# Adding adaLN's partial sums over partitions by accumulating transfers instead of TensorE matmuls

## The chip, the cores and the metric

The kernel runs on one core of a Trainium2 chip. The metric is the device time of one execution in microseconds. Before the change three runs took 1121.29 to 1122.57 us, with a median of 1122.05 us. Times inside an execution come from one profiled execution and are counted from the start of its span.

## What is computed

The kernel computes a two-layer trunk for 512 tokens of width 1024, all in float32. Layer 0 is stick-breaking attention and a SwiGLU FFN, layer 1 a gMLP token mixer and a second SwiGLU FFN. Each of the four sub-layers is wrapped in two RMS norms and in an adaLN modulation by one conditioning vector `c`:

```python
def ada_modulation(c, w, b):
    m = jax.nn.silu(c) @ w + b
    shift, scale, gate = jnp.split(m, 3, axis=-1)
...
    shift, scale, gate = ada_modulation(c, mix_ada_w[i], mix_ada_b[i])
    h = rms_norm(x, mix_pre_g[i]) * (1.0 + scale) + shift
    y = mixer(h)
    x = x + gate * rms_norm(y, mix_post_g[i])
```

So each sub-layer s needs three rows of 1024 numbers from `c`, each a product of a vector of 1024 with a 1024 x 1024 matrix. The code names them after the sub-layer whose residual they follow: G0 to G3 are the gates of sub-layers 0 to 3 (times `post_g`), A0 to A2 the scales (one plus scale, times `pre_g`) of sub-layers 1 to 3, and B0 to B2 their shifts. G0 belongs to attention, G1 to FFN 0, G2 to gMLP and G3 to FFN 1; A1 and B1 are used at the end of FFN 0 for gMLP's input, A2 and B2 at the end of gMLP for FFN 1's input. (The scale and shift of attention itself are made in another way, at the start.)

## The kernel before

**Matmuls.** Every float32 matrix is split into a high and a low part (`split`): ScalarE copies the high part to fp32r, VectorE subtracts it from the source. `mm3` (line 90 is the matmul in it) then does three matmuls, high by high, high by low, low by high. So each weight tile of 128 x 1024 goes by DMA into `raw`, through a copy on ScalarE (`wh`) and a subtraction on VectorE (`wl`), and activations go the same way (`as` in front of the projections back). Nearly all compute instructions on VectorE and ScalarE are recorded through one helper, so that they carry line 64.

**Stages.** Attention ends near 260 us of the span. FFN 0 follows: three plain units (`gu`), nineteen blocks by seven products instead of eight (`r`), then the projection back, `out_proj`, with 22 weights of `wdown` (`y`), of which the last four are the tail. gMLP comes next (`u` units, eight steps of `v` for each of two halves, the last four of the second half in the tail, the layer norm, three more `u` units, the mixing over positions `sv`, `out_proj`), and FFN 1 last, whose projection back is written out in `last` (`X`, `M`). At the end of each `out_proj`, `boundary` does for each of four token tiles the norm, the gate (`t<-y,G`), the residual, which POOL stores to DRAM (`xd`), and the next input (`t<-x,A`, then `t<-t,r,B`), which TensorE transposes (`tp`).

**The adaLN rows.** Class `Bg` makes the rows in the background, one step at a time, in between the steps of the stages. For each row, POOL clears an accumulator of 128 x 1024 and SP loads the bias into its first partition. Then eight times a slab of 128 x 1024 of the matrix is loaded (`rawada`) and VectorE adds it, scaled by the slab's part of silu(c), in one instruction (`ada_stt`). After this, the 128 partitions of the accumulator hold partial sums. They are added over the partitions, and the sum brought to all partitions, on TensorE: each half of 512 is split (`acch` on ScalarE, `accl` on VectorE), multiplied by a matrix of ones (`adaps`), and evacuated with the multiplication by a broadcast `pre_g` or `post_g`, or copied for B:

```python
split(h[:], l[:], acc[:, c])
...
ps = self.bank()
mm(ps[:], ones_r, h[:], True, False, last_tp[0])
mm(ps[:], ones_r, l[:], False, True)
```

Attention sums G0, A0 and B0 in that way with slabs that POOL loads. G1 is made in FFN 0's blocks and G3 in FFN 1's, with slabs in slots of the pool `s4`. A1, B1 and G2 are made in FFN 0's `out_proj`, two slabs a weight, with two slab buffers that they share with the FFN blocks' `rawy`. When their 24 slabs are through, at k = 13 (`mid`), the bank of token tile 0 is copied to SBUF (`yp`), so that `adaps` gets a bank, all three rows are added over partitions there, and token tile 0 begins anew in the bank; `yp` is added at its end. From k = 13 on the A2 and B2 object takes one step a weight, and it is finished in gMLP's `v` steps, two slabs a step.

**What sets the order.** Each engine runs its instructions in order, and so do the DMA queues of SP and POOL: an instruction whose wait is not over holds all behind it. From FFN 0 on no order is written out by hand for VectorE, ScalarE and SP. A scheduler of the tile framework sets it when the program is built, from the order of the code and from its own estimates. `Written.gate` and `order` add constraints to it.

Of the kernel before, what the change touches and what calls it, by code (L numbers as in the profile page):

```python
# [8 lines left out]
F32 = mybir.dt.float32  # L9
# [16 lines left out]
def trunk(ctx: ExitStack, tc: tile.TileContext, A: dict, out: bass.AP):  # L26
# [5 lines left out]
    adas = ctx.enter_context(tc.tile_pool(name="adas", bufs=1))  # L32
# [3 lines left out]
    dram = ctx.enter_context(tc.tile_pool(name="dram", bufs=1, space=bass.MemoryType.DRAM))  # L36
    psum = ctx.enter_context(tc.tile_pool(name="psum", bufs=1, space=bass.MemoryType.PSUM))

    uid = [0]
# [264 lines left out]
    lng = cols[:, 1, :]  # L304

    def ada_stt(acc, w, kk):
        dve.scalar_tensor_tensor(
            acc, w, sc[:, kk : kk + 1], acc, ALU.mult, ALU.add
        )

# [2 lines left out]
    class Bg:  # L313
# [4 lines left out]

        def __init__(self, *parts, slots=False, queue=nc.sync):
            self.slots = slots  # L320
            self.queue = queue
            self.bank = lambda: bank("adaps", "p")
# [15 lines left out]
        def run(self):  # L338
            for name, at, s, part in self.parts:
                acc = slot(F32, name, 1, D)[:, 0, :]  # L340
                ada[name, at] = acc
                nc.gpsimd.memset(acc, 0.0)
                load(acc[0:1, :], A["adab"][s, part], self.queue)
                for k in range(KD):
                    if self.slots:
                        raw = slot(F32, "rawada", 1, D)[:, 0, :]
                        load(raw, A["ada"][s, part, k])
                        yield
                    else:
                        self.ahead(1 + (k + 1 < KD or name != self.parts[-1][0]))  # L350
                        raw = self.raws.pop(0)
                    ada_stt(acc, raw, k)
                    if not self.slots:
                        yield
            for name, at, s, part in self.parts:
                acc = ada[name, at]
                if part:
# [3 lines left out]
                for b in range(2):  # L361
                    c = slice(b * 512, (b + 1) * 512)
                    h = adas.tile([P, 512], F32R, tag="acch", name=nm("acch"))
                    l = adas.tile([P, 512], F32R, tag="accl", name=nm("accl"))
                    split(h[:], l[:], acc[:, c])
                    yield
                    yield
                    ps = self.bank()
                    mm(ps[:], ones_r, h[:], True, False, last_tp[0])
                    mm(ps[:], ones_r, l[:], False, True)  # L370
                    if part == 0:
                        act.activation(acc[:, c], ps[:], AF.Copy)
                    elif part == 1:
                        dve.scalar_tensor_tensor(acc[:, c], ps[:], 1.0, g[:, c], ALU.add, ALU.mult)
                    else:
                        dve.tensor_tensor(acc[:, c], ps[:], g[:, c], ALU.mult)

        def step(self, n=1):

            while n and next(self.gen, self) is not self:  # L380
                n -= 1
            return n

    def rms(part, first=None):

# [104 lines left out]
        return t  # L490


    def out_proj(s, nk, get_act, wkey, J, bg, hT, nxt=(), pre=None, S=None, steps=0, bg2=None):

        last = 0 if steps else 3
        mid = min(nk - J, -(-8 * len(bg.parts) // steps) + 1) if steps else None  # L500
        yp = None
        y = [[None, None] for _ in range(NT)]

        def step(k, tt, a, w, halves=(0, 1)):
            for hf in halves:
                if k == 0 or k == mid and tt == last:
                    y[tt][hf] = bank("y", "p" if tt == last else "b")
                mm3(
                    y[tt][hf][:],
                    a[0][:, tt * P : (tt + 1) * P], a[1][:, tt * P : (tt + 1) * P],  # L510
                    w[0][:, 0, hf * 512 : (hf + 1) * 512],
                    w[1][:, 0, hf * 512 : (hf + 1) * 512],
                    k == 0 or k == mid and tt == last, k == nk - 1 or k + 1 == mid and tt == last,
                )

        npre = 0
# [26 lines left out]
        for tt in range(NT):  # L543
            for hf in range(2):
                for k, a, w in tail:
                    step(k, tt, a, w, (hf,))
            if tt == last and yp is not None:
                for hf in range(2):
                    dve.tensor_tensor(yp[:, hf, :], y[tt][hf][:], yp[:, hf, :], ALU.add)
                y[tt] = [yp[:, hf, :] for hf in range(2)]  # L550
# [208 lines left out]
    with tc.tile_pool(name="att", bufs=1) as att, tc.tile_pool(name="att2", bufs=6) as att2:  # L759
# [192 lines left out]
        bg.bank = None  # L952
        cur = attend(0)
        for k in range(KD):
            if k % 2 == 0:
# [18 lines left out]
        for i in range(NPAIR):  # L974
# [6 lines left out]
            def rest():  # L981
                n, sums = next(F)
                fill(n)
                bg.step(sums)

            for group, js in zip((LATE, *EARLY), (B31, B2, B0)):
                flip(group, 0)
# [11 lines left out]
                step_v(i - 2)  # L999
        for _ in fgen:  # L1000
            bg.step(1)
        bg.step(99)
        pe["chain"] = dve.chain = act.chain = False

# [14 lines left out]
    class Ffn:  # L1019
# [78 lines left out]

            return rest

        def run(self, bg0, bg, bg2, steps, nhT, nxt, nS=None):
            for f in range(NH):
                self.unit(f, 256, 256)()
            for f in range(NH, KF):
                self.seven(f)()
                if f % 3:
                    bg0.step(1)
            bg0.step(99)
            if self.li == 1:
                return self.last()  # L1110
            out_proj(
                self.s, KF, lambda k: act_split(self.act[k // 2][:, k % 2, :]),
                lambda k: ("wdown", self.li, k), 4, bg, nhT, nxt, None, nS, steps, bg2,
            )


        def last(self):
# [113 lines left out]
            for half in range(2):  # L1231
# [3 lines left out]
                tail = items[-NLAST:] if half else []  # L1235
                while n < len(items) and items[n][0] == half and items[n] not in tail:
                    ahead(n)
                    _, kind, j = items[n]
                    n += 1
                    if kind == "o":  # L1240
# [75 lines left out]
        return lambda: [e() for e in ev]  # L1316

    def gmlp(bg, hT, nhT, nS, nxt):
        wsr = wraw.tile([P, KD, P], F32, tag="raw", name="wsr")
        load(wsr[:], A["ws"])  # L1320
        nc.gpsimd.memset(wsr[0:64, :, 64:P], 0.0)
# [93 lines left out]
                    )  # L1415

        for m in range(KD):
            mix(m)
            sp.append(act_split(u4[m // 2][:, m % 2, :]))
            if m >= 4:  # L1420
# [12 lines left out]
    )  # L1433
    bg2 = Bg("A2", "B2")
    f0.run(
        Bg("G1", slots=True), Bg("A1", "B1", "G2"), bg2, 2, hT2,
        [lambda a=a: u_first(hT2, range(a, min(a + 2, NU))) for a in range(0, NU, 2)],
    )
    gmlp(bg2, hT2, hT3, S3, f1.first())
    f1.run(Bg("G3", slots=True), bg2, None, 0, None, ())  # L1440


def _layout(i):
# [82 lines left out]
```

## Time and profile before

| what | value |
|---|---|
| median of three runs | 1122.05 us |
| the profiled execution | 1123.81 us |
| its span | 1122.0 us |
| TensorE busy | 1104.4 us, 7318 matmuls |
| VectorE busy | 903.3 us, 1161 instructions |
| ScalarE busy | 603.4 us, 977 instructions |
| POOL busy | 39.8 us, 71 instructions |
| rawada loads on SP's queue | 56 of 512 KB, 4.7 us each from issue to landing |
| rawada loads on POOL's queue | 24 of 512 KB, 4.5 us each |

Matmuls are pipelined and their ends are modelled, so the length of one in a row is longer than the distance to the next one. PE is TensorE, PEld its weight loads, DVE VectorE, ACT ScalarE; SPq and POOLq are the queues on which SP and POOL issue DMAs. A row of a timeline has the start, the length, the engine, the line, the operation with its output and inputs by the program's names, and, in brackets, idle time before it and what ended that.

### The profile page before, as it was taken

What the parts mean: (1) busy time and instruction counts of PE and PEld (TensorE: products, weight loads), DVE (VectorE), ACT (ScalarE), POOL (GpSimd) and SP (SyncE); (2) the same over time, 40 slices, a digit from 0 to 9 for tenths busy, and PEclk for the clock granted to TensorE, in tenths of its full rate; (3) what the DMA queues carried; (4) which work ended last, traced back from release to release, by engine and by line L of the source; (5) the groups of instructions that cost most, each with busy time, mean ns of one, the idle gap of its engine ahead of it and who ended that gap; (6) DMA issues with size and microseconds to landing.
All of it is one profiled execution on the core that took longest, in us unless ns stands there. A gap on an engine that the chain in (4) does not pass through costs nothing.

```text
span 1122.0 us, 18286 instructions
## 1 busy us (share of the span) xinstructions
PE 1104.4 (98%) x7318; PEld 993.9 (89%) x7318; DVE 903.3 (81%) x1161; ACT 603.4 (54%) x977; POOL 39.8 (4%) x71
## 2 busy tenths in 40 slices
PE   6999999999999999999999999999999999999997
PEld 5788878779999999988878988989999999989896
DVE  7777889759998988797587774759988988889986
ACT  7646767646655555552244634437555555556552
POOL 0220111000000000010000000000000000000000
PEclk9999999999999999999999999999999999999999
DMA  9676445353344444278874582333244444223223
GB/s 358 229 228 169 142 147 160 135 188 132 106 125 147 151 148 122 90 243 264 272 255 167 182 286 80 110 129 134 77 151 140 128 133 147 76 75 113 95 96 149
DMA packets 51298, 176.09 MB, mean 157 GB/s; under 512 B 5643, under 2 KB 6155, under 8 KB 50318
## 3 DMA queue, kind: packets, MB, share of 16 engines
q1 hardware_dynamic: 45166, 153.95, 42.0%
q0 software_dynamic: 6048, 20.98, 6.0%
q8 instruction: 57, 0.93, 0.3%
q14 instruction: 27, 0.22, 0.1%
HBM read 164.43 MB, written 8.39 MB: 154 GB/s over the span
## 4 chain that ended last, share of the span: by engine, by line
PE 88%; DMA 6%; DVE 3%; ACT 2%; issue 1%; SPq 0%; DVEq 0%; ACTq 0%
PE r L90 33%; PE y L90 12%; PE X L90 7%; PE v L90 7%; PE pqk L90 7%; PE gu L90 6%; PE u L90 4%; DMA rawada<-in_ada 3%; PE M L90 3%; PE z L90 2%; PE av L90 2%; PE tw L98 2%; DMA raw<-in_wdown 1%; DMA ada<-in_ada0w 1%; PE tp L98 1%; PE sv L90 1%
## 5 line engine op out<-in xcount | busy, mean ns | idle before, releaser
L64 ACT ACTIVATE wh<-raw 128x1024 fp32r<-128x1024 f32 (+1 forms) x112 | 117.0, 1051 | 138.3 <-PE y L90 45.6
L64 DVE TENSOR_TENSOR wl<-raw,wh 128x1024 fp32r<-128x1024 f32 (+1 forms) x112 | 135.0, 1211 | 59.4 <-ACT wh L64 57.9
L90 PE MATMUL r<-Sh,wh 128*128 128x256 f32 x608 | 170.2, 280 | 0.3 <-ACT e L64 0.3
L90 PE MATMUL r<-Sh,wl 128*128 128x256 f32 x608 | 170.4, 280 | 0.0
L90 PE MATMUL r<-Sl,wh 128*128 128x256 f32 x608 | 170.1, 280 | 0.0
L90 PE MATMUL y<-wh,as 128*128 128x512 f32 x480 | 154.0, 398 | 0.0
L64 DVE TENSOR_TENSOR wl<-f,wh 128x1024 fp32r<-128x1024 f32 x76 | 92.8, 1220 | 35.8 <-ACT wh L64 35.8
L64 ACT ACTIVATE wh<-f 128x1024 fp32r<-128x1024 f32 x76 | 80.7, 1061 | 67.9 <-PE r L90 64.8
L90 PEld LDWEIGHTS r<-Sh,wh 128*128 128x128 f32 x608 | 114.7, 189 | 0.5 <-ACT e L64 0.5
L90 PEld LDWEIGHTS r<-Sl,wh 128*128 128x128 f32 x608 | 114.6, 189 | 0.0
L90 PEld LDWEIGHTS r<-Sh,wl 128*128 128x128 f32 x608 | 114.6, 189 | 0.0
L90 PEld LDWEIGHTS y<-wh,as 128*128 128x128 f32 x480 | 90.7, 189 | 21.3
L90 PE MATMUL y<-wl,as 128*128 128x512 f32 x240 | 95.5, 398 | 0.0
L90 PE MATMUL r<-hTh,wh 128*128 128x256 f32 x304 | 88.8, 293 | 0.0
L90 PE MATMUL r<-hTl,wh 128*128 128x256 f32 x304 | 84.8, 279 | 0.0
L90 PE MATMUL r<-hTh,wl 128*128 128x256 f32 x304 | 80.1, 280 | 0.0
L90 PE MATMUL X<-wh,as 128*128 128x512 f32 (+1 forms) x272 | 76.2, 356 | 0.0
L64 ACT ACTIVATE e<-r 128x256 f32<-128x256 f32 x114 | 43.4, 382 | 51.9 <-PE r L90 51.7
L90 PEld LDWEIGHTS r<-hTh,wh 128*128 128x128 f32 x304 | 57.2, 188 | 5.1 <-DVE gu L64 0.9
L90 PE MATMUL r<-hTh,b 128*128 128x256 f32 x304 | 60.7, 282 | 0.0
L64 ACT ACTIVATE wh<-rawx 128x1024 fp32r<-128x1024 f32 x38 | 40.4, 1062 | 36.5 <-PE r L90 30.8
L90 PEld LDWEIGHTS r<-hTl,wh 128*128 128x128 f32 x304 | 57.3, 188 | 0.1
(240 smaller groups left out, 2842.6 us busy)
## 6 DMA issues: line engine op xcount, KB each, us to landing
rawada<-in_ada SPq DMA_DIRECT2D x56, 512.0 KB, 4.7
raw<-in_wdown SPq DMA_DIRECT2D x44, 512.0 KB, 4.0
rawy<-in_wy SPq DMA_DIRECT2D x38, 512.0 KB, 3.6
rawx<-in_wx SPq DMA_DIRECT2D x38, 512.0 KB, 4.3
rawada<-in_ada POOLq DMA_DIRECT2D x24, 512.0 KB, 4.5
raw<-in_wqk SPq DMA_DIRECT2D x16, 512.0 KB, 4.2
ada<-in_ada0w SPq DMA_DIRECT2D x7, 1026.0 KB, 11.2
raw<-in_wgu SPq DMA_DIRECT2D x12, 512.0 KB, 3.5
```

Source lines behind the costliest of these rows:

```text
L64: b = f(*a, **k)
L90: b = nc.tensor.matmul(o, l, r, start=start, stop=stop, skip_group_check=True)
L98: last_tp[0] = nc.tensor.transpose(o, i, ident)
```

## The change

The code of `Bg` now keeps the matmuls for G0, A0 and B0 alone. When the last slab of any other row is added, a generator `total` is appended to a list `trees`; each call of `grow` takes every generator in it one step further. `total` adds partitions 64 to 127 onto 0 to 63 by a DMA that accumulates, then 32 to 63 onto 0 to 31, and so on: seven DMAs on POOL's queue, each of which needs the one before. Then VectorE multiplies the one row that is left in partition 0 by `pre_g` or `post_g` (not for B), and POOL writes the row to DRAM and loads it from there into all partitions.

Calls of `grow` are put where steps of the stages are: in `Bg.step`, in `run`, in `last`, in the mixing loop and in `out_proj`. With no `adaps` in FFN 0's `out_proj`, `mid`, `yp` and the second object (`bg2`) go from it: its steps are two slabs a weight for k < 8, one after that. A2 and B2 are summed in gMLP alone, behind the last `t<-t,r,B` of the boundary before (`bg.gate`). The pool `adas` of the split halves moves behind the others in SBUF.

```diff
-                    ada_stt(acc, raw, k)
+                    b = ada_stt(acc, raw, k)
+                    if self.gate is not None:
+                        order(b, self.gate)
+                    if k == KD - 1 and self.queue is nc.sync:
+                        trees.append(total(acc, s, part))
                     if not self.slots:
                         yield
+            if self.queue is nc.sync:
+                return
...
             while n and next(self.gen, self) is not self:
+                grow()
                 n -= 1
             return n
+
+    trees = []
+
+    def total(acc, s, part):
+
+        n = P // 2
+        while n:
+            nc.gpsimd.dma_start(out=acc[0:n, :], in_=acc[n : 2 * n, :], accum_op=ALU.add)
+            yield
+            n //= 2
+        if part:
+            g = slot(F32, "g", 1, D)[:, 0, :]
+            load(g[0:1, :], A["pre_g" if part == 1 else "post_g"][s : s + 1, :], nc.gpsimd)
+            yield
+            if part == 1:
+                dve.scalar_tensor_tensor(acc[0:1, :], acc[0:1, :], 1.0, g[0:1, :], ALU.add, ALU.mult)
+            else:
+                dve.tensor_tensor(acc[0:1, :], acc[0:1, :], g[0:1, :], ALU.mult)
+        row = dram.tile([1, D], F32, tag="row", bufs=4, name=nm("row"))
+        nc.gpsimd.dma_start(out=row[:], in_=acc[0:1, :])
+        yield
+        nc.gpsimd.dma_start(out=acc, in_=row[:].to_broadcast([P, D]))
+
+    def grow(n=1):
+
+        while n and trees:
+            trees[:] = [t for t in trees if next(t, trees) is not trees]
+            n -= 1
...
-            bg.step(steps)
-            if bg2 is not None and mid is not None and k >= mid:
-                bg2.step(1)
-            if k + 1 == mid:
-                yp = slot(F32, "yp")
-                for hf in range(2):
-                    act.activation(yp[:, hf, :], y[last][hf][:], AF.Copy)
-                bg.step(99)
+            bg.step(steps if k < KD else min(steps, 1))
+            if steps == 0:
+                grow()
...
     def gmlp(bg, hT, nhT, nS, nxt):
+        bg.gate = ready[0]
```

Three pieces of the order show what moves. The first is ScalarE's in FFN 0's `out_proj`; `raw` to `wh` are weights, `as` activation splits. Before, from the sixteenth to the eighteenth weight of `wdown`:

```order
L64 ACTIVATE wh_5661<-raw_5659 128x1024
L64 ACTIVATE wh_5749<-raw_5747 128x1024
L64 ACTIVATE wh_5792<-raw_5790 128x1024
L64 ACTIVATE yp_5695<-y_5180 128x512
L64 ACTIVATE yp_5695<-y_5184 128x512
L64 ACTIVATE as_5744<-act_4044 128x512
L64 ACTIVATE as_5787<-act_4294 128x512
L64 ACTIVATE as_5823<-act_4294 128x512
L64 ACTIVATE as_5859<-act_4544 128x512
L64 ACTIVATE as_5895<-act_4544 128x512
L64 ACTIVATE as_5931<-act_4798 128x512
L64 ACTIVATE as_5952<-act_4798 128x512
```

Now, from the ninth weight to the fourteenth; after these rows come weights alone up to the boundary:

```order
L64 ACTIVATE as_5840<-act_4544 128x512
L64 ACTIVATE wh_5385<-raw_5383 128x1024
L64 ACTIVATE as_5873<-act_4792 128x512
L64 ACTIVATE as_5894<-act_4792 128x512
L64 ACTIVATE as_5897<-act_5036 128x512
L64 ACTIVATE wh_5426<-raw_5424 128x1024
L64 ACTIVATE as_5900<-act_5036 128x512
L64 ACTIVATE wh_5467<-raw_5465 128x1024
L64 ACTIVATE wh_5512<-raw_5510 128x1024
L64 ACTIVATE wh_5553<-raw_5551 128x1024
L64 ACTIVATE wh_5590<-raw_5588 128x1024
```

The copies into `yp` and the splits of accumulators are gone, and the activation splits, of which seven stood in a row behind the eighteenth weight, are all through before the eleventh.

The second is POOL's in the same stage. Before, its instructions for A1, B1, G2 and A2 and the first store of the residual:

```order
L342 MEMSET A_5212 128x1024
L342 MEMSET B_5373 128x1024
L342 MEMSET G_5532 128x1024
L342 MEMSET A_5779 128x1024
L429 DMA xd_6006<-x_5962 128x1024
```

Now, from the middle of B1's tree (B_5369; A_5196 is A1, G_5540 is G2, `row` a row in DRAM):

```order
L395 DMA B_5369<-B_5369 32x1024
L407 DMA row_5504<-A_5196 16x1x64
L395 DMA B_5369<-B_5369 16x1024
L409 DMA A_5196<-row_5504 128x1024
L395 DMA B_5369<-B_5369 8x1024
L395 DMA B_5369<-B_5369 4x1024
L395 DMA B_5369<-B_5369 2x1024
L395 DMA G_5540<-G_5540 64x1024
L395 DMA B_5369<-B_5369 1x16x64
L395 DMA G_5540<-G_5540 32x1024
L407 DMA row_5769<-B_5369 16x1x64
L395 DMA G_5540<-G_5540 16x1024
```

B1's last addition stands behind G2's first one, which waits for G2's last slab; the stores of the residual stand behind all of G2's additions.

The third is VectorE's in gMLP, around the statistics of the layer norm (`bns`, `mv`); `wl` are weights. Before:

```order
L64 TENSOR_TENSOR wl_6803<-raw_6800,wh_6802 128x1024
L64 TENSOR_TENSOR accl_6751<-B_6583,acch_6750 128x512
L64 TENSOR_TENSOR wl_6809<-raw_6806,wh_6808 128x1024
L64 TENSOR_TENSOR wl_6905<-raw_6902,wh_6904 128x1024
L64 BN_STATS bns_6812<-vt_6524 128x6
L64 BN_AGGR mv_6813<-bns_6812 128x2
L64 BN_STATS bns_6812<-vt_6525 128x6
L64 BN_AGGR mv_6813<-bns_6812 128x2
L64 BN_STATS bns_6812<-vt_6526 128x6
L64 BN_AGGR mv_6813<-bns_6812 128x2
L64 TENSOR_TENSOR wl_6961<-raw_6958,wh_6960 128x1024
```

Now, with B2's sixth to eighth slabs and A2's multiply by `pre_g`:

```order
L64 SCALAR_TENSOR_TENSOR B_6603<-rawada_6653,sc,B_6603 128x1024
L64 TENSOR_TENSOR wl_6856<-raw_6853,wh_6855 128x1024
L64 SCALAR_TENSOR_TENSOR B_6603<-rawada_6657,sc,B_6603 128x1024
L64 BN_STATS bns_6763<-vt_6464 128x6
L64 SCALAR_TENSOR_TENSOR B_6603<-rawada_6673,sc,B_6603 128x1024
L64 BN_AGGR mv_6764<-bns_6763 128x2
L64 BN_STATS bns_6763<-vt_6465 128x6
L64 BN_AGGR mv_6764<-bns_6763 128x2
L64 SCALAR_TENSOR_TENSOR A_6502<-A_6502,g_6676 1x1024
L64 BN_STATS bns_6763<-vt_6466 128x6
L64 BN_AGGR mv_6764<-bns_6763 128x2
L64 TENSOR_TENSOR wl_6912<-raw_6909,wh_6911 128x1024
```

The last two slabs and the multiply now stand among the second half's statistics, where only weights stood.

More of the change, by code (lines that the diff above doesn't have):

```diff
@@ L31, in trunk @@
     wpool = ctx.enter_context(tc.tile_pool(name="wpool", bufs=5))
-    adas = ctx.enter_context(tc.tile_pool(name="adas", bufs=1))
     npool = ctx.enter_context(tc.tile_pool(name="npool", bufs=2))
@@ L36, in trunk @@
     dram = ctx.enter_context(tc.tile_pool(name="dram", bufs=1, space=bass.MemoryType.DRAM))
+    adas = ctx.enter_context(tc.tile_pool(name="adas", bufs=1))
     psum = ctx.enter_context(tc.tile_pool(name="psum", bufs=1, space=bass.MemoryType.PSUM))
@@ L306, in ada_stt @@
     def ada_stt(acc, w, kk):
-        dve.scalar_tensor_tensor(
+        return dve.scalar_tensor_tensor(
             acc, w, sc[:, kk : kk + 1], acc, ALU.mult, ALU.add
@@ L320, in __init__ @@
             self.slots = slots
-            self.queue = queue
-            self.bank = lambda: bank("adaps", "p")
+            self.queue, self.gate, self.turn = queue, None, 0
             self.parts = [
@@ L368, in run @@
                     ps = self.bank()
-                    mm(ps[:], ones_r, h[:], True, False, last_tp[0])
+                    mm(ps[:], ones_r, h[:], True, False)
                     mm(ps[:], ones_r, l[:], False, True)
@@ L490, in x_load, with out_proj @@
         return t
-    def out_proj(s, nk, get_act, wkey, J, bg, hT, nxt=(), pre=None, S=None, steps=0, bg2=None):
+    def out_proj(s, nk, get_act, wkey, J, bg, hT, nxt=(), pre=None, S=None, steps=0):
         last = 0 if steps else 3
-        mid = min(nk - J, -(-8 * len(bg.parts) // steps) + 1) if steps else None
-        yp = None
         y = [[None, None] for _ in range(NT)]
@@ L505, in step @@
             for hf in halves:
-                if k == 0 or k == mid and tt == last:
+                if k == 0:
                     y[tt][hf] = bank("y", "p" if tt == last else "b")
@@ L512, in step @@
                     w[1][:, 0, hf * 512 : (hf + 1) * 512],
-                    k == 0 or k == mid and tt == last, k == nk - 1 or k + 1 == mid and tt == last,
+                    k == 0, k == nk - 1,
                 )
@@ L546, in out_proj @@
                     step(k, tt, a, w, (hf,))
[L547 to L550, printed above, removed]
             if tt < 2:
@@ L983, in rest @@
                 fill(n)
-                bg.step(sums)
+                if bg.step(sums):
+                    grow()
             for group, js in zip((LATE, *EARLY), (B31, B2, B0)):
@@ L1001, in trunk @@
             bg.step(1)
+            grow()
         bg.step(99)
@@ L1099, in seven, with run @@
             return rest
-        def run(self, bg0, bg, bg2, steps, nhT, nxt, nS=None):
+        def run(self, bg0, bg, steps, nhT, nxt, nS=None):
             for f in range(NH):
@@ L1107, in run @@
                     bg0.step(1)
+                else:
+                    grow()
             bg0.step(99)
@@ L1112, in run @@
                 self.s, KF, lambda k: act_split(self.act[k // 2][:, k % 2, :]),
-                lambda k: ("wdown", self.li, k), 4, bg, nhT, nxt, None, nS, steps, bg2,
+                lambda k: ("wdown", self.li, k), 4, bg, nhT, nxt, None, nS, steps,
             )
@@ L1237, in last @@
                     ahead(n)
+                    grow()
                     _, kind, j = items[n]
@@ L1417, in gmlp @@
         for m in range(KD):
+            grow()
             mix(m)
@@ L1435, in trunk @@
     f0.run(
-        Bg("G1", slots=True), Bg("A1", "B1", "G2"), bg2, 2, hT2,
+        Bg("G1", slots=True), Bg("A1", "B1", "G2"), 2, hT2,
         [lambda a=a: u_first(hT2, range(a, min(a + 2, NU))) for a in range(0, NU, 2)],
@@ L1439, in trunk @@
     gmlp(bg2, hT2, hT3, S3, f1.first())
-    f1.run(Bg("G3", slots=True), bg2, None, 0, None, ())
+    f1.run(Bg("G3", slots=True), bg2, 0, None, ())
 def _layout(i):
```

1 line of the change is left out of this document (removed).

## The prediction

> **What bounds the kernel now.** I read the page's busy times first, then what TensorE waited for, then TensorE in order of time around the one wait that I found, then the chain behind that wait.
>
> ```profile
> span 1122.0 us, 18286 instructions
> PE 1104.4 (98%) x7318; PEld 993.9 (89%) x7318; DVE 903.3 (81%) x1161; ACT 603.4 (54%) x977; POOL 39.8 (4%) x71
> ```
>
> TensorE is busy 98% of the span, so a change pays by the matmuls that it takes from TensorE and by the waits that it ends there. The list of TensorE's waits has one in the middle of the kernel that belongs to the code that is changed, and the group view gives the matmuls that go:
>
> ```profile
> PE adaps L90 <- ACT acch L64: 2.0, 1, 2.0
> L90 PE MATMUL adaps<-acch,ones x14: 387/396/549, 465.7 to 996.7; 128*128 128x512 f32 x14
> L90 PE MATMUL adaps<-accl,ones x14: 392/392/628, 465.9 to 997.0; 128*128 128x512 f32 x14
> ```
>
> That is 7 rows (G1, A1, B1, G2, A2, B2, G3) by 2 halves by 2 matmuls, 28 in all. The 0.39 us of one is not what it costs: matmuls overlap. TensorE in order of time (start, length) in FFN 0's projection back shows the spacing, and the wait:
>
> ```profile
> 560.76 0.39 PE L90 MATMUL adaps<-acch,ones 128*128 128x512 f32 x1
> 560.99 0.40 PE L90 MATMUL adaps<-accl,ones 128*128 128x512 f32 x1
> 561.23 0.40 PE L90 MATMUL y<-wh,as 128*128 128x512 f32 x1
> ...
> 562.39 0.62 PE L90 MATMUL y<-wh,as 128*128 128x512 f32 x2
> 565.02 0.50 PE L90 MATMUL adaps<-acch,ones 128*128 128x512 f32 x1 [2.01 <-ACT acch L64]
> ...
> 569.00 0.63 PE L90 MATMUL y<-wh,as 128*128 128x512 f32 x2
> ```
>
> A 512-wide matmul starts 0.233 us after the one before it (560.76 to 561.23 is two). At 565.02 TensorE had stood 2.01 us, and from 565.02 to 569.00 ten matmuls start in 3.98 us, 0.40 each. The windows view says why: the clock column falls below 1.00 (columns: window, length, busy of PE, PEld, DVE, ACT and POOL, clock, DMA share, GB/s).
>
> ```profile
> 482.00:560.00 78.00, 78.00 (x362) 64.06 (x361) 57.92 (x57) 25.70 (x36) 2.87 (x3) 1.00 0.82 264
> 560.00:580.00 20.00, 17.99 (x71) 14.09 (x71) 18.60 (x25) 10.06 (x18) 0.00 (x0) 0.91 0.77 256
> ```
>
> The chain that ended last tells what the awaited `acch` stood behind on ScalarE: a weight that came late, two copies into `yp`, seven activation splits and one more weight.
>
> ```profile
> 550.39 1.23 DVE wl L64
> 551.64 6.09 DMA raw<-in_wdown
> 557.84 1.06 ACT wh L64
> 558.90 0.97 ACT yp L64 x2
> 559.87 3.27 ACT as L64 x7
> 563.40 1.05 ACT wh L64
> ```
>
> **What the change takes from TensorE.** 28 matmuls by 0.233 us are 6.5 us. The wait at 565.02 is a wait of a matmul that no longer exists: 2.01 us from the modelled end of the matmul before, and 0.17 us more since the next start normally falls before that end (0.40 long, 0.233 apart): 2.2 us. The slow stretch behind it costs 3.98 less 10 by 0.233, 1.65 us. Sum: 6.5 + 2.2 + 1.65 = 10.4 us.
>
> [...]
>
> What could be late next at that place are the weights and the activation splits. The split at 550.39 is the sixteenth of `wdown` in VectorE's order, for k = 15; TensorE starts k = 13 at 561.23 and takes 24 by 0.233 = 5.6 us for one k, so it wants k = 15 at 572: 20 us of lead. The activation splits now stand far ahead in ScalarE's order, all before the eleventh weight. So I put nothing in the place of this wait. The two adds into `yp` leave the boundary's chain as well, for which TensorE does not wait: nothing.
>
> **What it adds, and what hides it.** Each row gets seven dependent accumulating transfers on POOL's queue, a multiply on one partition (not B), a write to DRAM and a broadcast load. No accumulating transfer is in the trace. The nearest rows of POOL's queue, from issue to landing:
>
> ```profile
> A<-in_adab POOLq DMA_DIRECT2D x1, 4.0 KB, 2.4
> xd<-x POOLq DMA_DIRECT2D x12, 512.0 KB, 2.9
> after<-V POOLq DMA_DIRECT2D x4, 508.0 KB, 10.4
> g<-in_post_g SPq DMA_DIRECT2D x4, 512.0 KB, 7.3
> ```
>
> The bounds of one step are 2.4 and 10.4 us. I take 2.9: the steps have 256 KB falling to 4 KB, and only `after`, SBUF to SBUF as these are but queued five in a row behind a slab, is slow. A tree is then 7 by 2.9 = 20 us, and 2.9 + 7.3 = 10 us more until all partitions have the row. Nothing of it is on TensorE; the question is who is behind it on VectorE, which works in order. The rows that set the dates:
>
> ```profile
> 506.52 1.28 DVE L64 SCALAR_TENSOR_TENSOR A<-rawada,sc,A 128x1024 f32<-128x1024 f32 x1
> 533.66 1.28 DVE L64 SCALAR_TENSOR_TENSOR G<-rawada,sc,G 128x1024 f32<-128x1024 f32 x1 [0.64 <-DMA rawada<-in_ada]
> 555.15 1.28 DVE L64 SCALAR_TENSOR_TENSOR G<-rawada,sc,G 128x1024 f32<-128x1024 f32 x1 [1.15 <-DMA rawada<-in_ada]
> 606.16 1.28 DVE L64 SCALAR_TENSOR_TENSOR t<-t,r,B 128x1024 f32<-128x1024 f32 x1
> 1028.36 0.42 DVE L64 TENSOR_TENSOR tf<-tf,raw 128x256 f32<-128x256 f32 x1
> 1056.97 1.29 DVE L64 TENSOR_TENSOR K<-K,G 128x512 f32<-128x512 f32 x2
> ```
>
> A1: the last slab is added by 507.8, the multiply stands behind G2's first slab (534.9): 27 us for seven steps, 3.9 each. Behind it wait G2's slabs and the weights for k = 13 and on, with the 20 us of lead. B1: its last step stands on POOL behind G2's first, which waits for G2's last slab (556.4); a step, the row's write and the broadcast end near 556 + 2.9 + 2.9 + 7.3 = 570, wanted at 606 less the gain so far. G3's multiply stands behind the sum at 1028.36, 28 us ahead of its use, and the row's write and broadcast need 10. The x stores behind the trees on POOL are read a stage later. The memsets of the accumulators, for which SP's loads of `adab` wait, stand on POOL ahead of the trees of their stage. All these I cost at nothing; with a cover gone, each us late would be one of TensorE's. The multiply is no row of the trace: between a one-column operation and the 1.28 us of 128 partitions I take the latter; five of them replace ten evacuations and fourteen low-part splits, so VectorE and ScalarE have less to do.
>
> **The moved slabs.** A2 and B2 are now all summed in gMLP: sixteen slabs where eight were. Two buffers pace them. VectorE's rows of before for the eight and for the layer norm behind them, and TensorE's step that needs the norm (times here are before's):
>
> ```profile
> 644.88 2.60 DVE L64 SCALAR_TENSOR_TENSOR B<-rawada,sc,B 128x1024 f32<-128x1024 f32 x2
> 652.39 2.61 DVE L64 SCALAR_TENSOR_TENSOR B<-rawada,sc,B 128x1024 f32<-128x1024 f32 x2 [1.39 <-DMA rawada<-in_ada]
> 658.43 2.60 DVE L64 SCALAR_TENSOR_TENSOR B<-rawada,sc,B 128x1024 f32<-128x1024 f32 x2
> 665.08 2.60 DVE L64 SCALAR_TENSOR_TENSOR B<-rawada,sc,B 128x1024 f32<-128x1024 f32 x2 [0.80 <-DMA rawada<-in_ada]
> ...
> 688.60 0.69 DVE L64 BATCH_NORM_STATS2 bns<-vt 128x6 f32<-128x512 f32 x1 [1.11 <-ACT vt L64]
> 689.32 0.21 DVE L64 BATCH_NORM_AGGREGATE mv<-bns 128x2 f32<-128x12 f32 x1
> 698.05 1.21 DVE L64 TENSOR_TENSOR wl<-raw,wh 128x1024 fp32r<-128x1024 f32 x1
> 699.56 0.18 DVE L64 RECIPROCAL r<-sd 128x4 f32<-128x4 f32 x1 [0.30 <-ACT sd L64]
> 706.75 2.36 DVE L64 TENSOR_TENSOR vnl<-vt,vnh 128x1024 fp32r<-128x1024 f32 x2 [0.59 <-ACT vnh L64]
> ...
> 713.28 6.65 PE sv L90 x60
> ```
>
> Pairs come 6.73 us apart (20.20 by 3), and with one weight a pair, as at 533.66 to 555.15, 6.14 apart. Four gaps of the latter and three of the former put the eighth pair at 689.6, with one BN_STATS inside it to 692.9. In the order there follow A2's multiply, three more statistics, four aggregates and two weights (1.28 + 3 by 0.69 + 4 by 0.21 + 2 by 1.21 = 6.6 us), to the reciprocal at 699.5, where it was. The layer norm then ends at 709.1, and TensorE, eight matmuls (1.9 us) shorter here, wants it at 711.4: 2.3 us to spare. Cost nothing, thinly covered. A2's tree starts near 668, and its multiply stands behind the eighth pair: 25 us, 3.6 for a step.
>
> **Against the profiled execution** (1123.8, its span 1122.0) the sum gives 1113.4; that run was 1.75 above the median of the three (1122.05), so the median to expect is 1111.7.
>
> **Rivals.** First, the layer norm comes late. At the slowest distance of the rows, 7.5 us (644.88 to 652.39), the eighth pair ends at 700.7, the norm 7.7 us later than worked out, 5.4 beyond the cover; with a slow stretch of 1.65 us that takes 7 us back: 1118.7. For it: the cover is 2.3 us; against: the slab pace slows with the number of weights loaded between, and there are fewer. Chance 0.15.
>
> Second, the wait at 565 stays under another name, or was not in the timed runs: then only the matmuls count, 1115.5. For it: ScalarE waited for a weight there. Against: the lead of 20 us. Chance 0.08.
>
> Third, slower: the steps of the trees are slow. VectorE's multiply for A2 then holds the layer norm, and all of the lateness reaches TensorE. It costs from 3.6 us a step on; lateness is 7 by (d - 3.6) less 2.3 of cover, plus 1.65. At d = 5.2 the 10.4 us are spent; at d = 6 it is 16.8 - 2.3 + 1.65 = 16.2, so 1128; at 10.4 us the multiply for A1 breaks its lead of 20 us too (73 - 27 - 20 = 26), near 1185. For it: the row of `after`, the only transfer within SBUF, and that an accumulating one must read what it adds to. Against: the rows of 2.4 and 2.9. Chance 0.08. [...]
>
> That the matmuls don't go is none: the built program has 28 fewer.
>
> **The numbers.** Forecast 1111.7 at 0.66; with 0.15 and 0.08 for the first two rivals, 0.08 for the third, 0.03 left for small losses that leave no change. About 0.2%, 2.2 us, is what a measurement of this kernel can tell: faster is below 1119.8. The worst of the first rival lies near that, so faster 0.87, same 0.05, slower 0.08. The range reaches down by the spread of the runs (1121.3 to 1122.6) and the rounding of the terms to 1110, and up to the first rival's bulk, 1118; the third is left out.
>
> **What would show it.** Right: no `adaps` among TensorE's groups, no TensorE wait near 555 to 570, clock 1.00 in that window, `sv` straight behind `u`, POOL's accumulating transfers at 2.4 to 3.6 us. Wrong: TensorE waiting for VectorE at `sv`, VectorE waiting for a DMA at a one-partition multiply, or a tree longer than 25 us.

## The result and the profile after

The changed kernel took 1125.45 us in the median of 7 runs (1123.58 to 1128.82), the kernel before 1122.53 in 7 runs beside it (1121.29 to 1123.88). The ratio is 1.0026, 95% interval 1.0014 to 1.0038: slower by a quarter of a percent, where 1111.7 was forecast. The profiled execution took 1125.35 with a span of 1123.2, 1.2 above the span of before.

The page of the profile after, its first two lines:

```profile
span 1123.2 us, 18311 instructions
PE 1104.6 (98%) x7290; PEld 994.2 (89%) x7290; DVE 891.6 (79%) x1140; ACT 591.9 (53%) x957; POOL 89.3 (8%) x139
```

The 28 matmuls are gone (7318 to 7290), and yet TensorE is busy as long as before, 1104.6 us against 1104.4. A busy time that stays while the work shrinks says that some of the work ran slower. The lists of what TensorE and VectorE waited for (us in all, times, longest) name the place:

```profile
PE sv L90 <- DVE vnl L64: 3.9, 4, 2.1
...
DVE A L64 <- DMA A<-A: 13.9, 2, 7.9
```

The wait for `acch` is gone from TensorE's list, and with it the slow stretch at 565. The windows view (window, length, busy of PE, PEld, DVE, ACT and POOL, clock, DMA share, GB/s) has full clock there:

```profile
560.00:580.00 20.00, 20.00 (x88) 16.22 (x87) 9.80 (x8) 4.24 (x4) 4.50 (x6) 1.00 0.86 253
```

In its place stand four waits for the layer norm at `sv`, and on VectorE two waits of a one-partition multiply for its tree (A1's, 7.9 us, and A2's, 6.06). VectorE in order of time in gMLP, from the first pair of slabs to A2's multiply and the layer norm:

```profile
637.17 2.60 DVE L64 SCALAR_TENSOR_TENSOR A<-rawada,sc,A 128x1024 f32<-128x1024 f32 x2
...
685.75 1.28 DVE L64 SCALAR_TENSOR_TENSOR B<-rawada,sc,B 128x1024 f32<-128x1024 f32 x1 [1.06 <-DMA rawada<-in_ada]
...
687.95 1.28 DVE L64 SCALAR_TENSOR_TENSOR B<-rawada,sc,B 128x1024 f32<-128x1024 f32 x1 [0.31 <-DMA rawada<-in_ada]
...
689.94 0.21 DVE L64 BATCH_NORM_AGGREGATE mv<-bns 128x2 f32<-128x12 f32 x1
696.21 1.21 DVE L64 SCALAR_TENSOR_TENSOR A<-A,g 1x1024 f32<-1x1024 f32 x1 [6.06 <-DMA A<-A]
...
701.25 0.17 DVE L64 RECIPROCAL r<-sd 128x4 f32<-128x4 f32 x1
```

The last slab is added at 689.2, the multiply waits for its tree until 696.21, VectorE starts nothing else in the 6.06 us, and the rest of the layer norm stands behind it. TensorE in order of time at the same place:

```profile
703.47 0.33 PE L90 MATMUL sv<-wsh,vnh 128*128 128x128 f32 x1
...
704.91 0.33 PE L90 MATMUL sv<-wsh,vnl 128*128 128x128 f32 x1 [1.00 <-DVE vnl L64]
...
707.90 0.48 PE L90 MATMUL sv<-wsh,vnl 128*128 128x128 f32 x1 [2.06 <-DVE vnl L64]
...
709.52 0.48 PE L90 MATMUL sv<-wsh,vnl 128*128 128x128 f32 x1 [0.57 <-DVE vnl L64]
...
710.65 0.47 PE L90 MATMUL sv<-wsh,vnl 128*128 128x128 f32 x1 [0.23 <-DVE vnl L64]
...
721.16 0.73 PE L90 MATMUL y<-wh,as 128*128 128x512 f32 x1
...
725.04 0.22 PE L90 MATMUL sv<-wsh,vnh 128*128 128x128 f32 x1
```

And the same places in before's trace, with the start of `u`, which is at 611.97 in the trace after:

```profile
619.63 0.28 PE L90 MATMUL u<-hTh,wh 128*128 128x256 f32 x1
...
713.12 0.22 PE L90 MATMUL sv<-wsh,vnh 128*128 128x128 f32 x1
...
719.77 0.45 PE L90 MATMUL y<-wh,as 128*128 128x512 f32 x1
...
722.62 0.22 PE L90 MATMUL sv<-wsh,vnh 128*128 128x128 f32 x1
```

These rows give the account. At the first `sv` TensorE is 713.12 - 703.47 = 9.65 us ahead of before. From there to the second block of `sv` (725.04, 722.62) it takes 21.57 us where before took 9.50: 12.07 us lost. Behind that it gains 1.2 more, of which G3's four matmuls by 0.233 are 0.9; the rest is small differences in several places. Net: 9.65 - 12.07 + 1.2 = -1.2, the difference of the spans.

The 12.07 us are of two kinds. The twelfth `sv` starts at 710.65; eleven starts 0.111 apart (before's sixty, 713.12 to 719.77) behind 703.47 it would have been at 704.69: 5.96 us of lateness. The other 49 then take until 721.16, 10.51 us instead of 49 by 0.111 = 5.44, and the `y` behind them 3.88 instead of 2.85: 6.1 us of half clock. The windows view shows that clock:

```profile
700.00:708.00 8.00, 4.78 (x37) 4.30 (x35) 7.81 (x10) 5.91 (x7) 1.95 (x3) 0.90 0.75 222
708.00:714.00 6.00, 5.20 (x22) 4.76 (x22) 5.73 (x6) 5.30 (x7) 1.36 (x2) 0.50 0.49 128
714.00:718.00 4.00, 4.00 (x21) 4.00 (x20) 2.45 (x5) 1.26 (x2) 0.78 (x1) 0.50 0.86 300
718.00:724.00 6.00, 6.00 (x24) 5.43 (x24) 4.54 (x7) 1.26 (x2) 0.78 (x1) 0.55 0.28 110
```

0.50 from 708 to 718, ten microseconds, though TensorE has waited for nothing since 710.65.

The trees on POOL's queue, from the first step of each to the last (start, length of the issue, and in brackets the time for which POOL waited, with what ended it): G1, A1 and A2.

```profile
426.33 0.87 POOL L395 DMA_DIRECT2D G<-G  x1 [158.18 <-DVE gu L64]
...
450.05 0.77 POOL L395 DMA_DIRECT2D G<-G  x1 [3.62 <-DMA G<-G]
...
509.54 0.87 POOL L395 DMA_DIRECT2D A<-A  x1 [9.62 <-DVE A L64]
...
543.45 0.77 POOL L395 DMA_DIRECT2D A<-A  x1 [4.86 <-DMA A<-A]
...
662.56 0.88 POOL L395 DMA_DIRECT2D A<-A  x1 [23.63 <-DVE A L64]
...
692.80 0.78 POOL L395 DMA_DIRECT2D A<-A  x1 [3.73 <-DMA A<-A]
```

From the first step to the seventh are six steps: 3.95 us each in G1's tree, 5.65 in A1's, 5.04 in A2's. A2's whole tree, from 662.56 to the multiply at 696.21, is 33.65 us, 4.81 a step.

### The profile page after: what moved, and what is told of

Its sections match the earlier page's. It is cut to its first block, busy times and chain, and to the rows that moved or that the text cites. A ratio compares the mean times of both kernels' runs of the same rounds, so it can differ in the third digit from the quotient of the medians.

```text
span 1123.2 us, 18311 instructions
## 1 busy us (share of the span) xinstructions
PE 1104.6 (98%) x7290; PEld 994.2 (89%) x7290; DVE 891.6 (79%) x1140; ACT 591.9 (53%) x957; POOL 89.3 (8%) x139
## 4 chain that ended last, share of the span: by engine, by line
PE 95%; DVE 2%; DMA 1%; ACT 1%; SPq 0%; issue 0%; DVEq 0%
PE r L90 34%; PE y L90 19%; PE X L90 7%; PE v L90 7%; PE pqk L90 7%; PE gu L90 6%; PE u L90 4%; PE M L90 3%; PE z L90 2%; PE av L90 2%; PE tw L98 2%; PE sv L90 1%; DMA ada<-in_ada0w 1%; PE tp L98 1%; DVE ada L64 1%; PE pk L90 0%
```

## The experiments

The theory: the loss is A2's multiply. It stands ahead of the layer norm on VectorE and waits for a tree whose steps take 4.8 us instead of 2.9, and the half clock behind the waits doubles the price (6.1 us of it behind 5.96 of lateness). The rival: sixteen slabs make the layer norm late by themselves (the prediction's first rival). Two more questions hang on these: why a step takes 4.8, and what keeps the clock at half.

| kernel | median us (lowest to highest, runs) | ratio to before, 95% interval |
|---|---|---|
| e1_norm_first | 1114.51 (1113.34 to 1124.88, 12) | 0.9953 (0.9929 to 0.9976) |
| e2_price_matmuls | 1121.27 (1120.12 to 1128.82, 12) | 0.9999 (0.9982 to 1.0017) |
| e3_half_back | 1134.01 (1129.52 to 1134.77, 5) | 1.0094 (1.0071 to 1.0116) |
| e4_keep_warm | 1121.34 (1118.76 to 1124.45, 12) | 0.9987 (0.9974 to 1.0000) |
| e5_norm_alone | 1120.69 (1116.64 to 1123.73, 12) | 0.9979 (0.9965 to 0.9993) |
| e6_b2_first | 1116.24 (1113.52 to 1121.18, 6) | 0.9949 (0.9930 to 0.9967) |
| e7_no_add | 1122.19 (1113.15 to 1127.36, 10) | 0.9983 (0.9959 to 1.0008) |
| e8_dense_512 | 1126.49 (one run) | |
| e9_b2_first_u_late | 1117.08 (1112.84 to 1119.61, 6) | 0.9944 (0.9923 to 0.9965) |
| e10_b2_first_warm | 1116.88 (1115.71 to 1119.84, 6) | 0.9948 (0.9932 to 0.9963) |

**e1_norm_first.** The edit, with the layer norm's last VectorE instruction kept in `normed[0]`:

```diff
             if part == 1:
-                dve.scalar_tensor_tensor(acc[0:1, :], acc[0:1, :], 1.0, g[0:1, :], ALU.add, ALU.mult)
+                if s == 3:
+                    yield
+                b = dve.scalar_tensor_tensor(
+                    acc[0:1, :], acc[0:1, :], 1.0, g[0:1, :], ALU.add, ALU.mult
+                )
+                if s == 3:
+                    order(b, normed[0])
...
+        normed[0] = dve.prev
```

> The changed kernel with A2's one-partition multiply put behind the layer norm's last split on VectorE; nothing else moves, and A2's tree is as slow as before. Theory (the multiply, queued ahead of the layer norm, waits 6.06 us for the tree; TensorE is then 6 us late at sv and runs 6 us longer at half clock): the whole 12.1 us of that stretch come back, 1125.4 - 12.1 = 1113.3, between 1112 and 1115; no wait at sv, clock 1.00 from 700 to 740. Rival (sixteen slabs make the layer norm late by themselves): at most the multiply's own 1.2 us come back, about 1124.

Measured 1114.51 in the median, 10.9 below the change and 0.47% below before: the multiply's place is the cause, and the rival as it stood (about 1124) falls. But the runs are in two groups: eight from 1113.3 to 1116.0, four from 1120.9 to 1124.9. The clock, averaged over each execution, separates the same two groups: 0.997 to 0.999 in the eight, 0.991 to 0.994 in the four (in all seven runs of the change it was 0.989 to 0.992). The profiled run (1120.92) is one of the four, and its TensorE shows why:

```profile
705.09 0.33 PE L90 MATMUL sv<-wsh,vnl 128*128 128x128 f32 x1 [0.31 <-DVE vnl L64]
...
706.22 0.33 PE L90 MATMUL sv<-wsh,vnl 128*128 128x128 f32 x1 [0.58 <-DVE vnl L64]
```

```profile
708.00:714.00 6.00, 6.00 (x30) 6.00 (x30) 4.96 (x7) 1.70 (x3) 0.79 (x1) 0.50 0.78 204
```

Without any wait of the multiply, the layer norm still came late by 0.9 us of waits, and the half clock followed. So the rival is right in small: the cover of the layer norm is used up, in some runs. That the other three were late at the same place is read from their clock; only this one has a trace.

**e2_price_matmuls.** In a projection back, at k = 0:

```diff
+    DUP = 2
...
                 if k == 0:
                     y[tt][hf] = bank("y", "p" if tt == last else "b")
+                    for _ in range(DUP):
+                        mm(
+                            y[tt][hf][:], a[0][:, tt * P : (tt + 1) * P],
+                            w[0][:, 0, hf * 512 : (hf + 1) * 512], True, False,
+                        )
```

> e1_norm_first with 48 more 512-wide matmuls on TensorE: the first matmul of each of the 24 accumulations of a projection back is issued three times, which starts the sum anew and changes no value. Theory (TensorE is the bound and one such matmul costs the 0.233 us between two starts): 48 by 0.233 = 11.2 us above e1_norm_first, so 24 removed ones are worth 5.6. Rival (they fill time in which TensorE would wait anyway): under 4 us above e1_norm_first.

Measured 6.8 us between the medians: neither the 11.2 of the theory nor the rival's under 4. The traces tell where: against e1_norm_first the first `y` behind attention's sixteen is 1.8 us later (487.70 against 485.94), `u` behind FFN 0's sixteen 5.5 (617.74 against 612.26). FFN 0's sixteen cost 3.72, 0.233 each, as the prediction has it; attention's cost half of that, which suggests that about half of those stood where TensorE was not the bound. Twelve of the sixteen that the change took out ahead of `u` (A1's, B1's and G2's) stood in this projection back. gMLP's sixteen can't be read: both profiled runs have half clock there, for different lengths.

**e3_half_back.** In `out_proj`, to which the A2 and B2 object `bg2` is handed again:

```diff
-            bg.step(steps if k < KD else min(steps, 1))
+            if k < 12 or steps == 0:
+                bg.step(steps)
+            else:
+                bg2.step(2 if k < 14 else 1)
```

> The changed kernel with A2's eight slabs put back into FFN 0's projection back, as in the kernel before, and G2's two a weight again; the trees stay. A2's tree then starts some 60 us earlier and its multiply stands ahead of gMLP's first slab. Theory (only the multiply's wait hurts): 1112 to 1116. Rival (what hurts is that FFN 0's stage or gMLP's is too full of slabs, wherever they stand): above 1118.

Measured 1134.01: the theory's forecast for this kernel failed by 20 us. The loss has another place, three waits of TensorE in FFN 0's projection back, and on VectorE there:

```profile
PE y L90 <- DVE wl L64: 17.5, 3, 7.8
```

```profile
597.24 1.22 DVE L64 TENSOR_TENSOR wl<-raw,wh 128x1024 fp32r<-128x1024 f32 x1
605.57 1.21 DVE L64 TENSOR_TENSOR G<-G,g 1x1024 f32<-1x1024 f32 x1 [7.12 <-DMA G<-G]
606.72 2.34 DVE L64 TENSOR_TENSOR wl<-raw,wh 128x1024 fp32r<-128x1024 f32 x2
```

The longest of the three waits, 7.8 us, is the same mechanism at another row: G2's multiply now stands ahead of two weights and waits 7.12 us for its tree. The other two stand behind slabs that VectorE waits for. Before had the same slabs in this stage, summed by matmuls, and no waits of this size: the stage that was full enough for matmuls is too full with the trees and their multiplies, and here the rival is right too.

**e4_keep_warm.** In the first block of `sv`, ahead of the third matmul of each group:

```diff
             sv = bank("sv")
-            for n in range(NT):
+            if m == 0:
+                dum = bank("dum", "p")
+                for n, x in enumerate((4, 10, 5, 4)):
+                    o = sv[:, n * P : (n + 1) * P]
+                    h, l = [t[:, 0, :P] for t in vn[n]]
+                    mm(o, h, wsh[:, 0, :], True, False)
+                    mm(o, h, wsl[:, 0, :], False, False)
+                    for _ in range(x):
+                        mm(dum[:], ones_r, vn[0][0][:, 0, :512], True, True)
+                    mm(o, l, wsh[:, 0, :], False, True)
+            for n in range(NT if m else 0):
```

> The changed kernel with 23 matmuls that nobody reads (512 wide, 5.4 us at full clock) put between the first twelve of sv, where TensorE waits for the layer norm; the multiply stays where it is. Theory (of the 12.1 us lost, 6.0 are lateness and 6.1 the half clock behind it): the clock stays at 1.00, the lateness stays, and 5 to 6 us come back: 1119.4 to 1120.4. Rival (the loss is lateness alone and the half clock only a sign of it): 1125 or more.

The multiply still waited (3.90 us in its profile, less than the 6.06 of the change), and 23 matmuls more made the kernel 4.1 us faster in the median, 4.8 by the spans (1118.4 against 1123.2). The clock in the window in which the change had 0.66 (first the changed kernel, then e4_keep_warm):

```profile
700.00:720.00 20.00, 15.97 (x86) 15.05 (x85) 17.88 (x22) 12.51 (x16) 4.09 (x5) 0.66 0.69 217
```

```profile
700.00:720.00 20.00, 20.00 (x141) 18.50 (x140) 17.79 (x23) 12.55 (x15) 4.17 (x6) 1.00 0.71 211
```

The shorter wait could explain a part of the gain, so here are its first `sv` and the first of the second block:

```profile
705.44 0.22 PE L90 MATMUL sv<-wsh,vnh 128*128 128x128 f32 x1
...
720.31 0.22 PE L90 MATMUL sv<-wsh,vnh 128*128 128x128 f32 x1
```

That stretch takes 14.87 us, 5.37 above before's 9.50: the 23 matmuls by 0.233 and nothing else. In the change it was 12.07 above. The difference of 6.7 is the 6.1 us of half clock and 0.6 by which 5.37 is less than the lateness of 5.96; the spans differ by less, since TensorE came to `sv` 2 us later in this execution (705.44 against 703.47). So the half clock is a cost of its own; by the medians it is a little below the 5 to 6 us expected.

**e5_norm_alone.** To e1_norm_first:

```diff
+        vnh_last = act.prev
...
+            order(last_act[0], vnh_last)
...
+            act.gate = vnh_last
             w = wget(("wout", k), 2)
+            act.gate = None
```

> e1_norm_first, and ScalarE too does the layer norm's four splits before anything that was queued between them: a wout weight that waits for its DMA, a table load and one u evacuation; VectorE's low part of that weight goes behind the norm with it. e1_norm_first had 8 runs between 1113.3 and 1116.0 and 4 between 1120.9 and 1124.9, and its profile, one of the latter, shows TensorE waiting 0.9 us at sv and then half clock. Theory (those runs are the same lateness in small: the norm ends 1 us late, a wait of under 1 us is enough for the half clock, 6 us): all runs between 1112.5 and 1117. Rival (the two groups have another cause, or the norm is late from the slabs ahead of it): again about a third of the runs above 1120.

Neither: no two groups, but runs all the way from 1116.6 to 1123.7. The waits at `sv` are gone from its profile. A new one stands behind. The reading: a raw buffer comes free with its weight's split, so the weight after the one put off came later still, and it stands ahead of the first `u` on VectorE and the first `as` on ScalarE.

```profile
717.80 0.80 PE L90 MATMUL y<-wh,as 128*128 128x512 f32 x1 [4.73 <-ACT as L64]
```

```profile
714.11 1.06 ACT L64 ACTIVATE wh<-raw 128x1024 fp32r<-128x1024 f32 x1 [2.69 <-DMA raw<-in_wout]
717.12 0.63 ACT L64 ACTIVATE as<-u 128x512 fp32r<-128x512 f32 x1 [1.95 <-DVE u L64]
```

With ScalarE's order changed the `sv` waits were gone in this one profile, and this way of changing it gives the gain back behind them. That ScalarE's order alone made them is not shown.

**e6_b2_first.**

```diff
-    bg2 = Bg("A2", "B2")
+    bg2 = Bg("B2", "A2")
```

> The changed kernel with one word changed: B2's slabs ahead of A2's. B2's tree, which has no multiply, is the early one, and A2's multiply falls by itself behind the sixth of sv's evacuations on VectorE. Theory (it matters only that no multiply stands ahead of the layer norm): as e1_norm_first, most runs between 1113 and 1116, some at 1121 to 1125. Rival (a multiply that waits for its tree costs wherever it stands on VectorE): above 1118 in all runs.

Measured 1116.24, 0.9949 of before: one exchange turns the change from slower to faster by half a percent. B2's tree is now the early one, and no instruction ahead of the layer norm waits for it. The rival, above 1118 in all runs, falls. Its profiled run, the fastest of the six, has a span of 1111.4 and no wait at `sv`, 10.6 below before's 1122.0; the forecast's sum was 10.4. The median gains 5.7 (1121.98 was before's beside it), so the whole 10.4 came in the best run only. What spreads the others is not shown.

**e7_no_add.** In the tree:

```diff
-            nc.gpsimd.dma_start(out=acc[0:n, :], in_=acc[n : 2 * n, :], accum_op=ALU.add)
+            nc.gpsimd.dma_start(out=acc[0:n, :], in_=acc[n : 2 * n, :])
```

> The changed kernel with its tree transfers as plain copies of the same size and order, which leaves the sum over the partitions out of the seven rows. Theory (a step takes 4.8 us because each waits for the landing of the one before among transfers of weights and slabs, not because it adds): a step of A2's tree stays at 4.3 to 5.3 us and the time between 1122 and 1128. Rival (reading what it adds to is what makes it slow): a step near the 2.9 us of the x stores, and the time below 1117.

The step comes out between the two, and the median (1122.19) in the theory's range, but the runs are in two groups again: six from 1122.1 to 1127.4 at a mean clock of 0.991 to 0.993, four from 1113.2 to 1118.3 at 0.997 to 1.000. The profiled run (1115.79) is one of the four. A2's tree, first step and multiply in its trace:

```profile
664.48 0.53 POOL L395 DMA_DIRECT2D A<-A  x1 [25.06 <-DVE A L64]
```

```profile
691.99 1.21 DVE L64 SCALAR_TENSOR_TENSOR A<-A,g 1x1024 f32<-1x1024 f32 x1 [0.79 <-DMA A<-A]
```

27.5 us, 3.93 a step: of the 4.81, 0.9 is the adding (0.3 of it the issue on POOL, 0.51 us instead of 0.79). Of the two things that the theory blamed, the wait for the step before is not what costs the other 1.0; the transfers around it can be. G1's tree, in the quieter stage of FFN 0's blocks, has the same dependent copies:

```profile
427.04 0.54 POOL L395 DMA_DIRECT2D G<-G  x1 [158.84 <-DVE gu L64]
...
444.38 0.50 POOL L395 DMA_DIRECT2D G<-G  x1 [1.47 <-DMA G<-G]
```

Six steps in 17.34 us are 2.89 each, the price of the x stores. Counted in the same way, from the first step to the seventh:

| tree | plain copies, e7_no_add (DMA share) | accumulating, the change (DMA share) |
|---|---|---|
| G1 | 2.89 us a step (0.48) | 3.95 (0.59) |
| A2 | 4.05 (0.84) | 5.04 (0.86) |
| A1 | 4.94 (0.91) | 5.65 (0.88) |

Adding costs 0.7 to 1.1 us a step in each of the three, and the two stages with more DMA traffic cost 1.1 to 2.1 more in both kernels, with one execution of each. So two things made the step dear: the adding and the stage. In these three trees the time of a step rises with the DMA share; that it is the traffic of the stage, and not something else in which the stages differ, was not tested.

The 6 us that A2's tree gains this way bring its multiply to 0.79 us of wait: the edge of the cover.

**e8_dense_512.** Behind the first twelve of `sv`:

```diff
+            if m == 1:
+                for _ in range(12):
+                    mm(dum[:], ones_r, vn[0][0][:, 0, :512], True, True)
```

> The changed kernel with twelve 512-wide matmuls that nobody reads behind the first twelve of sv, where TensorE no longer waits. Theory (at half clock 128-wide matmuls, however close, don't bring the clock back, since the array works in half of their time; 512-wide ones do): the clock column is back at 1.00 within 4 us of the first of the twelve, and the 48 matmuls of sv behind them start 0.111 apart, not 0.213; about 1125. Rival (the clock comes back only a fixed 12 to 18 us after the wait, whatever runs): the 48 still 0.213 apart, about 1129.

```profile
713.16 4.79 PE L90 MATMUL dum<-vnh,ones 128*128 128x512 f32 x12
717.79 0.22 PE L90 MATMUL sv<-wsh,vnh 128*128 128x128 f32 x1
...
723.10 0.45 PE L90 MATMUL y<-wh,as 128*128 128x512 f32 x1
```

The twelve take 4.63 us, and the 48 `sv` behind them 5.31, 0.111 each: full clock, and the clock column has 1.00 from 718 to 724. In the changed kernel 49 `sv` at the same place had not brought it back in 10.5 us. The rival, a fixed 12 to 18 us, falls: full clock is back 7.7 us behind the end of the longest wait (710.07). The theory holds, with a single run (1126.49, about the 1125 expected).

**e9_b2_first_u_late.** To the changed kernel:

```diff
-    bg2 = Bg("A2", "B2")
+    bg2 = Bg("B2", "A2")
...
+        vnh_last = act.prev
...
+            order(last_act[0], vnh_last)
```

> e6_b2_first, with ScalarE's first u evacuation and its table load put behind the layer norm's fourth split; the wout weights stay where they are, unlike in e5_norm_alone. Theory (runs at 1121 are those in which the norm ends up to 1 us too late and the half clock follows; the evacuation ahead of the last two splits is 1.9 us of that): the median between 1112.5 and 1115.5 and at most one run in eight above 1119. Rival (the lateness comes from the slabs' transfers ahead of the norm, which this does not touch, or the u evacuations are wanted where they are): as e6_b2_first, median near 1116 and a run in six above 1119, or worse.

Measured 1117.08, two of six runs above 1119: it can't be told from e6_b2_first, and the theory's closer group did not come. In its profiled run A2's multiply waits 0.73 us at its new place, and a `y` of TensorE waits 1.82 us for VectorE behind it; this place has little cover too.

**e10_b2_first_warm.** To e6_b2_first, ahead of the second to fourth group of the first block of `sv`:

```diff
+                if m == 0 and n:
+                    for _ in range(4):
+                        mm(dum[:], ones_r, vn[0][0][:, 0, :512], True, True)
```

> e6_b2_first with twelve 512-wide matmuls that nobody reads, four ahead of each of the second to fourth group of three in sv's first twelve: 12 by 0.233 = 2.8 us of work that fills any wait there. Theory (what spreads the runs is the half clock after a short wait): all runs in a narrow group at e6_b2_first's lower end plus 2.8, 1115.5 to 1118.5, none above 1120. Rival (the spread has another cause): as wide as e6_b2_first, 1116 to 1124.

Measured 1116.88, 1115.7 to 1119.8, none above 1120 and one above the 1118.5 expected. The group is narrower than e6_b2_first's (4.1 us against 7.7, six runs each), at 2.8 us of work, and the median the same. That the half clock makes part of the spread fits; six runs don't show it. Here the mean clock is 0.996 to 0.999; in e6_b2_first five runs have 0.996 to 0.999 and the slowest, 1121.18, has 0.992.

What beats both kernels: e1_norm_first, e6_b2_first, e9 and e10 each lie some 0.5% below before, and can't be told from each other.

## Why the prediction was wrong, point by point

**What the matmuls and the old wait were worth: right.** By `u` sixteen matmuls, the wait and the slow stretch should have given 16 by 0.233 + 3.85 = 7.6 us; `u` starts 619.63 - 611.97 = 7.66 earlier. By `sv` eight matmuls more, 9.4; it was 9.65. Nothing took the place of the wait at 565: the clock from 560 to 580 is 1.00.

**The failed step: the price of a tree step,** "I take 2.9". In A2's tree it was 4.81 and in A1's 5.2 (36.2 us from 509.54 to its multiply), always inside the bounds of 2.4 and 10.4. The row that I took was that of plain stores at the boundaries, where the DMA share is 0.41 (598 to 618 us of the changed kernel); these steps add, and run at shares of 0.86 and 0.88. e7_no_add showed that 2.9 is right for a plain dependent copy in G1's quieter stage (2.89), that adding costs about 1 us more, and that the steps in the stages of A1 and A2 cost another 1 to 2. Waiting for the step before is hardly a cost of its own: from issue to landing, as the x stores are timed, the seven transfers of A2's tree took 6.7, 4.4, 4.6, 4.2, 3.9, 4.2 and 3.1 us, 31.1 of its 33.65.

**The third rival had the mechanism, and missed the half clock.** It said that VectorE's multiply for A2 would hold the layer norm, and gave this 0.08. With d = 4.8 its formula gives 7 by (4.8 - 3.6) - 2.3 = 6.1 us late; measured 5.96. That it is so close is luck: the tree had 27.6 us (662.56 to 690.15, when VectorE was free for the multiply), 3.9 a step and not 3.6, and the cover of 2.3 was gone (6.06 of wait made 5.96 of lateness); the two errors cancel. For the clock the formula adds 1.65, the stretch behind the wait at 565, where 512-wide matmuls follow. At `sv` 128-wide ones follow, and it was 6.1. With that, the step at which the 10.4 us are spent is not 5.2 but 3.6 + (10.4 + 2.3 - 6.1) / 7 = 4.5. Both sizes together turned a gain of 10 into a loss of 1.2; with the clock's price as I had it, d = 4.8 would have left 1119.5.

**A1, B1, G2, G3: right.** A1's tree took 36.2 us where 27 were given, its multiply waited 7.9 us, and the lead of 20 us covered that: no `y` stands in TensorE's list of waits.

**The moved slabs: the cover of 2.3 us was not there.** The slabs did move up with TensorE: `u` starts 7.66 us earlier, and the first pair at 637.17 where before had its first at 644.88, 7.71 earlier. But their pace was slower than the prediction's. The eighth pair starts at 685.75, so the seven gaps are 6.94 us each; the prediction had 6.14 for four and 6.73 for three, 6.39 in the mean, and its first rival 7.5. By the prediction's dates, moved up by 7.66, that pair would have ended at 685.2; it ended at 689.2, 4.0 us later. VectorE waited for slabs in both halves, 0.3 to 3.0 us a time. e1_norm_first showed what cover is left without the multiply: by their clock enough in eight runs, and 0.9 us short in the profiled one. So the first rival was right in kind, with half of its slower pace.

**The signs that I named** came as "wrong": TensorE waiting for VectorE at `sv`, VectorE waiting for a DMA at a one-partition multiply, a tree of over 25 us.

## What to carry to other kernels

An instruction with a small cost of its own that waits for a chain of transfers must not stand ahead of a short deadline where the engine starts nothing else meanwhile, as VectorE did not in 6.06 us: put it behind (one `order`, or another order of the rows), and price each link by a transfer that does the same work in a stage with as much traffic: here one step cost 2.9 us as a plain copy in a quiet stage (DMA share 0.48) and 5.0 to 5.7 as an addition in a busy one (0.86 to 0.88). A cover of 2 us that rests on a pace over seven gaps is none when the pace is off by 0.55 us. In two traces waits on TensorE cost themselves and a slow clock behind them: 1.65 us behind the wait of 2.01 in before, with 512-wide matmuls there, and 6.1 behind the waits at `sv` in the change, with 128-wide ones.

## What the runs showed of the hardware

**Once the clock was lost, 128-wide matmuls did not bring it back.** After the waits at `sv` the changed kernel ran 49 of them without a gap for 10.5 us, 0.213 apart, at clock 0.50; twelve 512-wide ones brought it back within 4.63 us (e8_dense_512). In e1_norm_first 128-wide ones ran so for 8.3 us (707.42 to 715.75). At half clock 512-wide ones start 0.426 apart (ten from 716.28 to 720.54 in e1_norm_first), so that 128 columns of them take 0.107, a quarter, by estimate: a 128-wide one every 0.213 fills half of the time. That this half is the reason is an inference from these distances and was not tested.

**At `sv` waits of under 1 us lost the clock in one trace and not in another.** e1_norm_first lost it after 0.31 and 0.58 us (0.50 from 708 to 714); with no wait before's sixty `sv` kept it for 6.65 us (1.00 from 700 to 720). e7_no_add kept it after 0.61 and 0.59:

```profile
700.00:720.00 20.00, 18.80 (x138) 17.44 (x138) 16.10 (x20) 12.05 (x15) 3.71 (x7) 1.00 0.53 175
```

Why two runs with nearly the same waits differ is not shown.

**An accumulating transfer** between partitions took 0.7 to 1.1 us a step more than a plain copy of the same shape (the table at e7_no_add), and its issue held POOL 0.79 us, against 0.51.
